# The samples' attention between a state-space stage: where its tiny copies run

## The chip, the cores and the metric

One NeuronCore of one Trainium2 chip runs the kernel. The metric is the device time of one execution in microseconds. The kernel before takes 1613.56 us, the median of three runs (1612.72 to 1615.05).

Engine names as in the profile: PE is the matrix engine (PEld its weight loads), DVE the vector engine, ACT the scalar engine, POOL the general engine (GpSimd), SP the engine that only starts transfers. Each engine runs its own instructions strictly in order; they wait for one another through semaphores.

## The reference

The kernel computes one layer of a decoder trunk for a prompt of 1024 positions and for 8 sample sequences of one new position each. What matters here is the samples' attention over 1024 cached positions (8 pages of 128) and the state-space branch beside it:

```python
z = q @ k.T * HEAD_DIM ** -0.5 + sb_bias         # 16 heads of 64 dims, keys in pages
log_w = log_beta + reverse_cumsum(log_keep) - log_keep   # stick-breaking, no softmax
o_att = exp(log_w) @ v

bu = einsum("gpc,bsgc->bsgp", bb, u)             # 64 groups, complex state of 64
x  = associative_scan(affine, (abar, bu))        # along the 1024 positions
y  = einsum("gcp,bsgp->bsgc", c, x) + d_skip * u
g  = gelu(y)
y_ssm = (g * sigmoid(g @ w_glu + b_glu) * silu(gate)) @ w_ssm_out

merged = sigmoid(m_att) * y_att + sigmoid(m_ssm) * y_ssm
x <- LayerNorm(alpha * x + gate(c) * (merged @ w_out))
```

Everything is float32; a product of matrices is made of three passes with split operands (ahi by whi, alo by whi, ahi by wlo).

## The kernel before

The program is in stages. First come the modulation, the projections and the prompt's attention (to some 715 us). Then the **state-space stage** (to about 1130 us): PE goes through the remaining column blocks of the input projection (`pj`, L141), and between them works on the eight feature blocks of the state-space branch. For each feature block, `take` (L970) has ACT evacuate the SSM input u out of PSUM in three chunks; two `inputs` matmuls (`sps`) are evacuated by ACT into the state tiles sr and si (L999, L1000); `recur` has DVE rotate them and run eight scans in place (L1028), and form xs (L1037); PE multiplies xs (`yp`, L1048); and `gelu` (L1080 to L1085) goes back and forth: ACT makes gh, gq and the polynomial's factor (L1080 to L1082), DVE the product gq·gh (L1083), ACT the tanh (L1084), DVE the result yy (L1085). There are two gelus to a feature block. Gate chunks (L1520) are evacuated by ACT too. After it come the merge, the gated linear unit and the projection `ssm_out` (to about 1340 us), the attention's output projection, and the finish.

The **samples' attention** is spread through the state-space stage. `SampleAttention.todo` is a list of small steps, and `tick` takes a few off it at each step of PE's work. K comes in 16 tiles of eight dims by four pages, V in eight tiles; a tile is `s_t`, of which there are two buffers. A "load" step is a pacing copy of one column into the tile (L805) and then four indirect transfers that POOL starts (L807). A K step handles two dims: two tiny copies make the factor tile s_q (L818, L819), and two operations (L828) add page times factor into the scores s_sc. A V step copies the pacing column into the accumulator (L815) and does two weighted sums (L823).

**Pacing.** `k.last` is a column of whatever the stage wrote last: u, sr, gin or the gelu's gh in the state-space stage. A copy from it makes the step depend on that work, so that a scheduler, which orders the instructions of each engine except PE by a simulated timeline, cannot put the step before it. PE's order is written out by hand. SP starts most weight loads; POOL starts the page loads, and makes the low parts of weights (wlo, L109).

The **late values** (`LateValues`, from some 1184 to 1337 us) are the part of the samples' V pages that are left for later: 32 tiles l_t, four buffers, loaded two steps ahead. `load` is a pacing copy from the column l_p (L865) and an indirect transfer by POOL (L866); each step then multiplies the tile (L884) and reduces it (L885) on DVE. At the end DVE adds the pages' sums (L888) and ACT's queue stores the result as d_o, which is read back as `orow` (L1283) and transposed by PE (L1285).

Of the kernel before, what the change touches and what calls it, by code (L numbers as in the profile page):

```python
# [9 lines left out]
F32 = mybir.dt.float32  # L10
# [136 lines left out]
class Stream:  # L147
# [33 lines left out]
    def one(self):  # L181

        if self.cur is None and self.begun:
            self.cur, self.n = self.begun.popleft()
        if self.cur is None:
            if not self.jobs:
                return False
            self.cur, self.n = gemm(self.k, *self.jobs.popleft()), 0
        next(self.cur)
        self.n += 1  # L190
        self.left -= MM
        self.clock += MM
        last = self.n == KT * 9
        if last:
            self.cur = None
            self.k.w.ensure()
        self.due()
        return None if last else True
# [41 lines left out]
def modulate(k, sp, ps, io, tabs):  # L240
# [28 lines left out]
    def turn(g):  # L269
# [7 lines left out]
        for i in range(2):  # L277
# [4 lines left out]
            k.act_h.append(split_act(k, k.hp, x))  # L282

    load(0)
    bc = sp.tile([128, 16], F32, name="bc", bufs=1)
    SP.dma_start(bc, io["bc"])
# [6 lines left out]
    k.w.stage.append(k.w2)  # L293
    k.w.ensure()
    load(1)
    next(tabs)
    load(2)
    SP.dma_start(k.ident, io["ident"])
    SP.dma_start(k.hb, io["sb_bias"].broadcast_to((128, H)))
# [447 lines left out]
class SampleAttention:  # L747
# [50 lines left out]
    def one(self, what, hf=0, c=0, d0=0):  # L798
        k, nc, pool = self.k, self.k.nc, self.pool
        DVE = nc.vector  # L800
        if what == "load":
            what, hf, c = hf, c, d0
            self.tiles.append(pool.tile([128, 4, 8, 128], F32, tag="s_t", bufs=2, name="s_t"))
            tile = self.tiles[-1]
            DVE.tensor_copy(tile[:, 0, 0, 0:1], k.last)  # L805
            for j in range(4 if what == "k" else VP):
                nc.gpsimd.indirect_dma_start(  # L807
                    out=tile[:, j].rearrange("p d s -> p (d s)"), out_offset=None, in_=self.io["cache_" + what],
                    in_offset=bass.IndirectOffsetOnAxis(ap=self.idx[:, 4 * hf + j, c:c + 1], axis=0))
        elif what in "kv":  # L810
            pages = 4 if what == "k" else VP
            sc = self.sc[:, 4 * hf:4 * hf + pages]
            dd = 8 * c + d0
            if what == "v":
                DVE.tensor_copy(self.acc[:, hf, dd:dd + 1], k.last)  # L815
            else:
                q = pool.tile([128, 2], F32, tag="s_q2", bufs=2, name="s_q2")
                DVE.tensor_copy(q[:, 0:1], k.last)  # L818
                DVE.tensor_copy(q, self.q[:, dd:dd + 2])  # L819
            for d in range(d0, d0 + 2):  # L820
                t, dd = self.tiles[0][:, 0:pages, d], 8 * c + d
                if what == "v":
                    DVE.scalar_tensor_tensor(t, t, 1.0, sc, op0=ALU.mult, op1=ALU.mult,  # L823
                                             accum_out=self.acc[:, hf, dd:dd + 1])
                elif dd == 0:
                    DVE.tensor_scalar(sc, t, q[:, 0:1], None, op0=ALU.mult)
                else:
                    DVE.scalar_tensor_tensor(sc, t, q[:, d - d0:d - d0 + 1], sc, op0=ALU.mult, op1=ALU.add)  # L828
            if d0 == 6:
                self.tiles.popleft()  # L830
        elif what == "w":
            n = PPS * 128
            ke = pool.tile([128, n], F32, tag="s_t", bufs=2, name="s_ke")
            sc = self.sc.rearrange("p j s -> p (j s)")
            nc.scalar.activation(ke, sc, AF.Sigmoid, bias=self.bias[:, 1:2], scale=-0.125)
            nc.scalar.activation(sc, sc, AF.Sigmoid, bias=self.bias[:, 0:1], scale=0.125)
            rev = ke[:, ::-1]
            DVE.tensor_tensor_scan(rev, rev, k.zcol.broadcast_to((128, n)), 1.0, ALU.mult, ALU.add)
            DVE.tensor_tensor(sc[:, 0:n - 1], sc[:, 0:n - 1], ke[:, 1:n], ALU.mult)
            nc.sync.dma_start(k.d_sc, sc[:, 128 * VP:])  # L840
        else:
            nc.sync.dma_start(k.d_acc, self.acc[:, 0])


class LateValues:
# [16 lines left out]
    def load(self, j, c):  # L862
        k, nc = self.k, self.k.nc
        t = self.ld.tile([128, 8, 128], F32, tag="wc", bufs=4, name="l_t")
        nc.vector.tensor_copy(t[:, 0, 0:1], k.last)  # L865
        nc.gpsimd.indirect_dma_start(  # L866
            out=t.rearrange("p d s -> p (d s)"), out_offset=None, in_=self.io["cache_v"],
            in_offset=bass.IndirectOffsetOnAxis(ap=self.idx[:, VP + j, c:c + 1], axis=0))
        self.tiles.append(t)
# [320 lines left out]
class Merge:  # L1190
# [77 lines left out]
    def open_a(self):  # L1268

        k, nc = self.k, self.k.nc  # L1270
        self.a_guard = self.pool("seta", "right")
        pa = self.a_guard.__enter__()
        self.act_a = []

        def one(f):
            t = self.load(k.d_a[f, 0], "x", NP)
            o, s = (self.ld.tile([128, NP], F32, tag="wc", bufs=4, name=n) for n in ("olo", "sga"))
            nc.sync.dma_start(o, k.d_a[f, 1])
            nc.sync.dma_start(s, k.d_sa[f])
            nc.vector.tensor_tensor(t[:, 0:NP], t[:, 0:NP], o, ALU.add)  # L1280
            nc.vector.tensor_tensor(t[:, 0:NP], t[:, 0:NP], s, ALU.mult)
            ob = self.ld.tile([NS, 128], F32, tag="orow", bufs=2, name="orow")
            nc.sync.dma_start(ob, k.d_o[:, blk(f)])  # L1283
            tp = k.psg.tile([128, 512], F32, tag="g", name="otp")
            nc.tensor.transpose(tp[:, 0:NS], ob, k.ident[0:NS, 0:NS])  # L1285
            nc.vector.tensor_tensor(t[:, NP:NT], tp[:, 0:NS], k.sgs[:, f], ALU.mult)
            self.act_a.append(split_act(k, pa, t))

        return [(110, None, lambda f=f: one(f)) for f in range(KT)]
# [429 lines left out]
```

## Time and profile before

| | |
|---|---|
| median of three runs | 1613.56 us (1612.72 to 1615.05) |
| the profiled execution | 1617.42 us, its span 1615.7 us |
| mean granted clock of PE | 0.969 |
| busy: PE, DVE, POOL, ACT | 1489.5, 1218.9, 911.0, 736.5 us |
| pacing and factor copies of the samples' attention on DVE | L805 24, L818 64, L819 64 |
| pacing copies of the late values on DVE | L865 32 |
| score operations L828 | 126 in 114.0 us, mean 905 ns |

In the profile's rows "out<-in" are tile names, and a bracket gives the idle time of the engine just before the row and what ended it: "[8.72 <-ACT u L970]" says that the engine stood for 8.72 us until ACT's instruction of line 970 on tile u was done. A row of the waits gives their total in us, their number and the longest. A row of a group of one form gives the duration's minimum, median and maximum in ns, then the first and last start.

### The profile page before, as it was taken

The numbers are of one execution on the slowest core, as the hardware profiler recorded it, in microseconds if no ns is written. First come the engines' busy times: TensorE is split into PE (matmuls) and PEld (weight loads), VectorE is DVE, ScalarE is ACT, GpSimd is POOL, SyncE is SP. The second block draws the span as 40 slices with busy tenths as digits, with TensorE's granted clock in tenths as the row PEclk, the third lists the DMA queues.
The fourth block names the chain that finished last, engine by engine and source line by source line (L and its number), as shares of the span: only waits on it lengthen the run. The fifth ranks groups of instructions, "written<-read, shape, count | busy, mean of one in ns | idle before, by whom it ended". The sixth has DMA issues, their size and how long they took to land.

```text
span 1615.7 us, 25524 instructions
## 1 busy us (share of the span) xinstructions
PE 1489.5 (92%) x9321; PEld 1410.2 (87%) x9321; DVE 1218.9 (75%) x1717; ACT 736.5 (46%) x1360; POOL 911.0 (56%) x744
## 2 busy tenths in 40 slices
PE   8899999999999999999989978889979786999997
PEld 4789999999999998999888978889779685899885
DVE  5558888888888888743899978787489975744566
ACT  3557777777776776643433333333432212311200
POOL 1738787878777877766566555552176541132164
PEclk9899999999999999999999989999989997999999
DMA  9323433334343434348789887875546677954322
GB/s 356 111 82 89 104 100 97 99 97 113 87 113 93 115 88 111 101 123 288 246 266 287 265 265 249 285 235 132 164 158 222 213 249 261 348 180 140 118 79 91
DMA packets 176731, 275.47 MB, mean 170 GB/s; under 512 B 46395, under 2 KB 119867, under 8 KB 176477
## 3 DMA queue, kind: packets, MB, share of 16 engines
q1 hardware_dynamic: 150555, 180.40, 36.6%
q0 software_dynamic: 23456, 84.95, 16.4%
q10 hardware_dynamic: 2594, 8.49, 2.0%
q8 instruction: 73, 1.20, 0.3%
q14 instruction: 53, 0.43, 0.1%
HBM read 196.77 MB, written 66.24 MB: 163 GB/s over the span
## 4 chain that ended last, share of the span: by engine, by line
PE 49%; DVE 26%; DMA 9%; issue 5%; ACT 3%; POOL 2%; SPq 1%; DVEq 0%; ACTq 0%; POOLq 0%
PE pj L141 32%; PE f L1397 6%; DVE s_sc L828 4%; PE o L700 3%; PE z L654 3%; PE tp L683 3%; DVE ke L665 3%; DVE l_t L884 2%; DMA s_t<-in_cache_k,s_idx 2%; DVE be L666 2%; DVE vs L636 2%; DMA l_t<-in_cache_v,l_idx 2%; DVE l_acc L885 2%; DVE wlo L109 1%; DVE xs L1037 1%
## 5 line engine op out<-in xcount | busy, mean ns | idle before, releaser
L141 PE MATMUL pj<-ahi,whi 128*128 128x344 f32 x2112 | 695.4, 331 | 36.8 <-ACT u L970 17.5
L141 PE MATMUL pj<-alo,whi 128*128 128x344 f32 x2112 | 686.1, 326 | 7.9 <-DVE alo L1220 4.1
L141 PE MATMUL pj<-ahi,wlo 128*128 128x344 f32 x2112 | 581.6, 328 | 6.0 <-POOL wlo L109 6.0
L141 PEld LDWEIGHTS pj<-ahi,whi 128*128 128x128 f32 x2112 | 405.6, 192 | 45.9 <-ACT u L970 18.3
L141 PEld LDWEIGHTS pj<-alo,whi 128*128 128x128 f32 x2112 | 405.6, 192 | 11.9 <-DVE alo L235 4.9
L141 PEld LDWEIGHTS pj<-ahi,wlo 128*128 128x128 f32 x2112 | 382.6, 192 | 8.0 <-POOL wlo L109 6.5
L665 DVE TENSOR_TENSOR_SCAN ke<-ke,eye 128x896 f32<-128x896 f32 (+7 forms) x128 | 217.7, 1701 | 92.4 <-ACT ke L655 92.2
L109 POOL TENSOR_TENSOR wlo<-w,whi 128x1024 fp32r<-128x1024 f32 x53 | 141.6, 2672 | 207.7 <-ACT whi L108 178.8
L108 ACT CAST whi<-w 128x1024 fp32r<-128x1024 f32 x90 | 94.9, 1055 | 137.3 <-PE pj L141 100.1
L655 ACT ACTIVATE ke<-z,nhb 128x448 f32<-128x448 f32 (+2 forms) x192 | 111.8, 582 | 81.1 <-PE z L654 79.2
L666 DVE TENSOR_TENSOR be<-be,ke 128x896 f32<-128x896 f32 (+7 forms) x128 | 128.0, 1000 | 13.0 <-ACT wthi L686 0.5
L828 DVE SCALAR_TENSOR_TENSOR s_sc<-s_t,s_q,s_sc 128x512 f32<-128x512 f32 x126 | 114.0, 905 | 18.0 <-DMA s_t<-in_cache_k,s_idx 12.0
L656 ACT ACTIVATE be<-z,hb 128x448 f32<-128x448 f32 (+2 forms) x192 | 110.6, 576 | 0.0
L807 POOL DMA_INDIRECT s_t<-in_cache_k,s_idx x64 | 70.6, 1103 | 50.8 <-DVE s_sc L828 15.5
L683 PE MATMUL tp<-ident,be 128*128 128x128 f32 x576 | 88.9, 272 | 0.0
L493 POOL TENSOR_TENSOR pt<-tab 128x256 f32<-128x256 f32 x64 | 79.5, 1241 | 3.1
L492 POOL TENSOR_TENSOR pr<-tab 128x256 f32<-128x256 f32 x32 | 25.9, 811 | 89.4 <-DMA tab<-d_tab 78.7
L1520 ACT ACTIVATE gate<-pj 128x344 f32<-128x344 f32 x72 | 32.7, 458 | 95.4 <-PE pj L141 86.5
L109 DVE TENSOR_TENSOR wlo<-w,whi 128x1024 fp32r<-128x1024 f32 x37 | 62.5, 1689 | 15.4 <-ACT whi L108 15.3
L686 ACT CAST wthi<-tp 128x512 fp32r<-128x512 f32 x96 | 56.7, 590 | 32.3 <-PE tp L683 29.9
L654 PE MATMUL z<-kl,qs 128*128 128x448 f32 (+2 forms) x192 | 66.0, 344 | 4.0 <-DMA kl<-kl 4.0
L687 DVE TENSOR_TENSOR wtlo<-tp,wthi 128x512 fp32r<-128x512 f32 x96 | 65.3, 680 | 5.7 <-ACT wthi L686 5.7
(314 smaller groups left out, 2758.5 us busy)
## 6 DMA issues: line engine op xcount, KB each, us to landing
w<-in_w_in SPq DMA_DIRECT2D x38, 512.0 KB
w<-in_w_in POOLq DMA_DIRECT2D x26, 512.0 KB, 5.6
wc<-in_w_cond SPq DMA_DIRECT2D x24, 512.0 KB
d_a<-ox SPq DMA_DIRECT2D x128, 64.0 KB
gst<-d_gg SPq DMA_DIRECT2D x8, 576.0 KB
x<-in_xr SPq DMA_DIRECT2D x9, 512.0 KB
xt<-in_xt SPq DMA_DIRECT2D x8, 516.0 KB
d_sg<-gate SPq DMA_DIRECT2D x8, 516.0 KB
```

Source lines behind the costliest of these rows:

```text
L108: nc.scalar.copy(whi, w32)
L109: self.eng.tensor_tensor(wlo, w32, whi.bitcast(F32), ALU.subtract)
L141: PE.matmul(ps[c], w[:, blk(t)], x[:, cs(c)], start=(t == 0 and i == 0), stop=(t == KT - 1 and i == 2))
L493: POOL.tensor_tensor(t1, c, d, ALU.mult)
L654: nc.tensor.matmul(z[:, 0:wide], st["q", h][:, blk(i)], x[:, s:s + wide], start=j == 0, stop=j == 1)
L655: nc.scalar.activation(ke[:, s:s + cw], z[:, 0:cw], AF.Sigmoid, bias=k.nhb[:, hd:hd + 1], scale=-0.125)
L656: nc.scalar.activation(be[:, s:s + cw], z[:, 0:cw], AF.Sigmoid, bias=k.hb[:, hd:hd + 1], scale=0.125)
L665: nc.vector.tensor_tensor_scan(rev, rev, self.eye[:, NP - n:][:, ::-1], 0.0, ALU.mult, ALU.add)
L666: nc.vector.tensor_tensor(be, be, ke[:, 1:n + 1], ALU.mult)
L683: PE.transpose(tp[:, 2 * order[a] + e], w[e][:, blk(2 * j + a)], k.ident)
L828: DVE.scalar_tensor_tensor(sc, t, q[:, d - d0:d - d0 + 1], sc, op0=ALU.mult, op1=ALU.add)
L1397: PE.matmul(pp[c], a[:, token(i)], w[:, blk(c, 512)], start=(t == 0 and a is ah and w is wh), stop=(t == KT - 1 and a is al))
```

## The change

Three kinds of tiny copies change engine. The pacing copies at page loads, in `SampleAttention.one` and in `LateValues.load`, are made by POOL, which also starts the transfers behind them. The factor copies are made by ACT, and the factor tile holds eight dims (one tile of K) instead of two, still with two buffers, so that the factors of up to 16 dims can stand ready. Nothing of what is computed changes.

```diff
-            DVE.tensor_copy(tile[:, 0, 0, 0:1], k.last)
+            nc.gpsimd.tensor_copy(tile[:, 0, 0, 0:1], k.last)
             for j in range(4 if what == "k" else VP):
                 nc.gpsimd.indirect_dma_start(
...
             else:
-                q = pool.tile([128, 2], F32, tag="s_q2", bufs=2, name="s_q2")
-                DVE.tensor_copy(q[:, 0:1], k.last)
-                DVE.tensor_copy(q, self.q[:, dd:dd + 2])
+                if d0 == 0:
+                    self.q8 = pool.tile([128, 8], F32, tag="s_q2", bufs=2, name="s_q2")
+                q = self.q8[:, d0:d0 + 2]
+                nc.scalar.copy(q[:, 0:1], k.last)
+                nc.scalar.copy(q, self.q[:, dd:dd + 2])
...
     def load(self, j, c):
         k, nc = self.k, self.k.nc
         t = self.ld.tile([128, 8, 128], F32, tag="wc", bufs=4, name="l_t")
-        nc.vector.tensor_copy(t[:, 0, 0:1], k.last)
+        nc.gpsimd.tensor_copy(t[:, 0, 0:1], k.last)
```

Since the scheduler orders anew, instructions that the diff doesn't name move as well. Lines of the changed kernel from 820 on are those of before plus two. PE's order is the same in both.

**DVE, around the two gelus of the fourth feature block.** s_q_10718 before, and s_q_10682 of the change, are the factors of the same new tile of K. Before:

```order
L1083 TENSOR_TENSOR gq<-gq,gh 128x512
L828 SCALAR_TENSOR_TENSOR s_sc<-s_t,s_q_10625,s_sc 128x512
L828 SCALAR_TENSOR_TENSOR s_sc<-s_t,s_q_10641,s_sc 128x512
L1085 SCALAR_TENSOR_TENSOR yy<-gq,gh 128x512
L828 SCALAR_TENSOR_TENSOR s_sc<-s_t,s_q_10641,s_sc 128x512
L805 COPY s_t<-gh 128x1
L818 COPY s_q_10718<-gh 128x1
L818 COPY s_q_10734<-gh 128x1
L819 COPY s_q_10718<-s_q 128x2
L819 COPY s_q_10734<-s_q 128x2
L828 SCALAR_TENSOR_TENSOR s_sc<-s_t,s_q_10718,s_sc 128x512
L1083 TENSOR_TENSOR gq<-gq,gh 128x512
```

The change, same place:

```order
L1085 TENSOR_TENSOR gq<-gq,gh 128x512
L830 SCALAR_TENSOR_TENSOR s_sc<-s_t,s_q_10510,s_sc 128x512 x2
L1087 SCALAR_TENSOR_TENSOR yy<-gq,gh 128x512
L830 SCALAR_TENSOR_TENSOR s_sc<-s_t,s_q_10510,s_sc 128x512 x2
L1085 TENSOR_TENSOR gq<-gq,gh 128x512
L830 SCALAR_TENSOR_TENSOR s_sc<-s_t,s_q_10682,s_sc 128x512
L1087 SCALAR_TENSOR_TENSOR yy<-gq,gh 128x512
```

The second product (L1083, now L1085) stood behind the first operation on the new tile and now stands ahead of it. In the fifth feature block the order before is the same (L1083 behind the first operation with s_q_11203), and the change there reads:

```order
L1085 TENSOR_TENSOR gq<-gq,gh 128x512
L830 SCALAR_TENSOR_TENSOR s_sc<-s_t,s_q_11004,s_sc 128x512 x2
L1087 SCALAR_TENSOR_TENSOR yy<-gq,gh 128x512
L1085 TENSOR_TENSOR gq<-gq,gh 128x512
L830 SCALAR_TENSOR_TENSOR s_sc<-s_t,s_q_11158,s_sc 128x512
```

There too the second product precedes the first operation on the new tile, whose factors are s_q_11158.

**ACT, the fourth feature block of the change**, from the last evacuations of the state tiles to the first gelu. Before, none of the rows L820 and L821 was there:

```order
L1001 COPY sr<-sps 64x272
L1002 COPY si<-sps 64x272
L1522 ACTIVATE gate<-pj 128x344 x2
L108 CAST whi<-w_10389 128x1024
L1522 ACTIVATE gate<-pj 128x344
L820 COPY s_q_10342<-sr 128x1 x4
L821 COPY s_q_10342<-s_q 128x2 x4
L1522 ACTIVATE gate<-pj 128x344 x2
L108 CAST whi<-w_10545 128x1024
L1522 ACTIVATE gate<-pj 128x344
L939 COPY gin<-tp 128x512
```

Eight copies, four of which read sr, stand between two groups of gate evacuations. sr is also what DVE's scans write.

On POOL a row L805 now stands ahead of the four L807 of each page load, and in the late values a row L867 ahead of each transfer L868, where before the copies stood in DVE's order.

## The prediction

> **What bounds the kernel now.** I read the page first (busy time and chain), then busy time by stage, then the waits of the stage that the change edits, then the timelines around the largest of them.
>
> ```profile
> PE 1489.5 (92%) x9321; PEld 1410.2 (87%) x9321; DVE 1218.9 (75%) x1717; ACT 736.5 (46%) x1360; POOL 911.0 (56%) x744
> PE 49%; DVE 26%; DMA 9%; issue 5%; ACT 3%; POOL 2%; SPq 1%; DVEq 0%; ACTq 0%; POOLq 0%
> ```
>
> TensorE (PE) bounds the whole, and VectorE (DVE) carries a quarter of the chain that ended last. The average hides two different stages. The rows below are 50 us each, busy time of PE, PEld, DVE, ACT and POOL, then the granted clock and the DMA share; the first two lie in the state-space stage with the samples' attention between it, the last two in the stage of the late values.
>
> ```profile
> 900.00:950.00 50.00, 41.28 (x268) 40.15 (x267) 40.15 (x79) 15.83 (x30) 28.73 (x29) 0.90 0.81 262
> 950.00:1000.00 50.00, 45.88 (x300) 44.75 (x299) 43.38 (x79) 20.11 (x37) 23.74 (x24) 0.97 0.77 251
> 1200.00:1250.00 50.00, 49.06 (x302) 48.78 (x303) 49.41 (x53) 12.21 (x17) 32.86 (x19) 0.97 0.60 198
> 1250.00:1300.00 50.00, 36.61 (x207) 35.67 (x206) 47.77 (x58) 12.17 (x17) 24.35 (x15) 0.86 0.66 214
> ```
>
> In the first two PE is busy 41 to 46 of 50 us and DVE 40 to 43, so PE is held up by single waits there, not by a full DVE; ScalarE (ACT) has 30 us free in each. In the late stage DVE is full (49.4, 47.8) and PE is what waits. The waits between 700 and 1100 us, engine, what waited, for whom, total, times, longest:
>
> ```profile
> PE pj L141 <- ACT u L970: 17.5, 4, 8.7
> PE yp L1048 <- DVE xs L1037: 9.9, 4, 3.5
> ACT gq L1084 <- DVE gq L1083: 60.2, 14, 8.7
> ```
>
> PE's largest wait is for ACT's evacuation of the SSM input u (L970), and two of its four times make 12.84 of the 17.5 us. What stands behind them is seen on three engines:
>
> ```profile
> 922.70 1.01 POOL L807 DMA_INDIRECT s_t<-in_cache_k,s_idx  x1 [1.61 <-DVE s_q L819]
> 929.30 0.72 ACT L1082 ACTIVATE gq<-gq,g 128x512 f32<-128x512 f32 x1
> 936.40 0.75 DVE L828 SCALAR_TENSOR_TENSOR s_sc<-s_t,s_q,s_sc 128x512 f32<-128x512 f32 x1 [5.46 <-DMA s_t<-in_cache_k,s_idx]
> 937.07 0.80 DVE L1083 TENSOR_TENSOR gq<-gq,gh 128x512 f32<-128x512 f32 x1
> 937.90 0.63 ACT L1084 ACTIVATE gq<-gq 128x512 f32<-128x512 f32 x1 [7.87 <-DVE gq L1083]
> 940.04 0.66 PE L141 MATMUL pj<-ahi,whi 128*128 128x344 f32 x1 [8.72 <-ACT u L970]
> 944.46 0.32 PE L141 MATMUL pj<-ahi,whi 128*128 128x344 f32 x1
> 944.62 0.32 PE L141 MATMUL pj<-alo,whi 128*128 128x344 f32 x1
> ```
>
> ACT had the factor of the second gelu ready at 930.02. DVE's product for it (L1083) stood behind the first score step of a page that landed at 936.4, since its load could start only at 922.7 when the tile came free. So DVE idled 5.46 us with the product queued, ACT stood 7.87 us with u behind it, and PE idled 8.72 us. After that the matmuls run slow: the 14 from 940.04 to 944.46 take 4.42 us where the pitch of the next two, 0.16 us, would make 2.2, another 2.2 us lost. One cycle later the same happens again:
>
> ```profile
> 980.45 0.72 ACT L1082 ACTIVATE gq<-gq,g 128x512 f32<-128x512 f32 x1
> 985.52 0.75 DVE L828 SCALAR_TENSOR_TENSOR s_sc<-s_t,s_q,s_sc 128x512 f32<-128x512 f32 x1 [4.29 <-issue]
> 986.19 0.68 DVE L1083 TENSOR_TENSOR gq<-gq,gh 128x512 f32<-128x512 f32 x1
> 986.90 0.63 ACT L1084 ACTIVATE gq<-gq 128x512 f32<-128x512 f32 x1 [5.73 <-DVE gq L1083]
> 989.04 0.65 PE L141 MATMUL pj<-ahi,whi 128*128 128x344 f32 x1 [4.12 <-ACT u L970]
> 992.28 0.31 PE L141 MATMUL pj<-ahi,wlo 128*128 128x344 f32 x1
> ```
>
> Here PE loses 4.12 us, and the 11 matmuls up to 992.28 take 3.24 us where 1.76 would do: 1.5 more.
>
> **The change part by part.** It takes 152 tiny copies off DVE in this stage (24 at L805, 64 at L818, 64 at L819) and 32 in the late stage (L865). Minimum, median and maximum in ns:
>
> ```profile
> L818 DVE COPY s_q<-sr x22: 122/142/155, 751.8 to 969.7; 128x1 f32<-128x1 f32 x22
> L819 DVE COPY s_q<-s_q x64: 151/162/2353, 739.7 to 990.6; 128x2 f32<-128x2 f32 x64
> L865 DVE COPY l_t<-l_p x32: 134/142/154, 1184.4 to 1323.5; 128x1 f32<-128x1 f32 x32
> L972 ACT COPY us_s<-pj x8: 213/232/267, 664.6 to 1041.5; 128x8 f32<-128x8 f32 x8
> L1038 POOL COPY xf<-xs x8: 183/192/667, 777.6 to 1116.3; 128x8 f32<-128x8 f32 x8
> 922.46 0.15 DVE L805 COPY s_t<-gin 128x1 f32<-128x1 f32 x1
> 922.53 0.16 DVE L819 COPY s_q<-s_q 128x2 f32<-128x2 f32 x1
> 922.60 0.15 DVE L818 COPY s_q<-gin 128x1 f32<-128x1 f32 x1
> ```
>
> A copy's row says 0.14 to 0.16 us, but in sequence they start 0.07 us apart (922.46, 922.53, 922.60), and up to 0.12 where one waits on the other. So 152 of them are 11 to 18 us of DVE's time, about 15, spread over 350 us that are not full: as plain relief they are worth little. The nearest rows for them elsewhere are 0.232 us on ACT and 0.192 us on POOL, for 8 elements; below lies DVE's 0.07. I take the upper ones: 128 × 0.232 = 29.7 us on ACT, and 56 × 0.192 = 11 us on POOL, both engines with room.
>
> The Trainium skill ("VectorE: DVE Perf Modes", the section on the TRN2 errata) speaks against this trade: it gives a ScalarE operation on SBUF a fixed 224 cycles at 1.2 GHz and a VectorE one 58 at 0.96 GHz, an estimate of 0.19 against 0.06 us, so that ACT pays three times what DVE saves. The rows agree (0.232 against a pitch of 0.07). By it the relief is 9 us rather than 15 and the sum about 1 us worse.
>
> *The two gelu stalls.* What the change does on the path is order (the listings in the section on the change show it). With the copies gone, the second product stands in DVE's new order ahead of the score step that waits for the page, in both cycles. First cycle: DVE is free at about 930.4, so product done 931.1; in the rows above PE starts 2.14 us after ACT takes L1084 (940.04 − 937.90), so PE starts at about 933.2 instead of 940.04: 6.8 us less. The four factor copies that stand on ACT ahead of L1084 fall into the time in which it waits for DVE. Second cycle: L1082 ends at 981.17, product at 981.9, u evacuated by 984.0; PE was ready at 984.92: all 4.12 us go. With the slow matmuls (2.2 + 1.5) that is 6.8 + 4.1 + 3.7 = **−14.6 us**. Bounds: 0 if PE only meets the wait later, −16.5 if all goes. The page still lands at 936.4; what is late next is the score steps themselves, and the next scan queued behind them.
>
> On the slow matmuls the Trainium skill ("TensorE: Matmul & The Clock Gate", the part on the HAM clock gate) says the array falls to half its rate after an idle window of about 3.4 us. The trace agrees: after 8.72 and 4.12 us the pitch was 0.29 us, and it came back within 4.4 and 3.2 us. By that rule a remaining wait of 1.9 us costs only itself, as the sum has it.
>
> *Waits of PE for xs* (9.9 us, 4 times): four to eight copies stood ahead of each xs on DVE, 0.3 to 0.9 us a time: **−2 us** (0 to −5).
>
> *New on ACT.* Copies stand between the chunks of u and, where the pacing value is the state tile sr, ahead of the gate evacuations; such a copy waits until DVE's scan has written sr. The rows are the scans of sr as a group (minimum, median, maximum in ns), then in one cycle the four scans and the gate chunk that will stand behind the copies:
>
> ```profile
> L1028 DVE TENSOR_TENSOR_SCAN sr<-r,sr x32: 390/394/2876, 763.2 to 1107.8; 128x128 f32<-128x128 f32 x32
> 903.44 3.94 DVE L1028 TENSOR_TENSOR_SCAN sr<-r,sr 128x128 f32<-128x128 f32 x4
> 910.45 0.46 ACT L1520 ACTIVATE gate<-pj 128x344 f32<-128x344 f32 x1 [8.17 <-PE pj L141]
> ```
>
> The scan ends at 907.38, eight copies later (1.9 us) it is 909.3, and the gate was due at 910.45: it just fits. Between the chunks of u two to four copies cost 0.3 to 0.9 us a time. Together **+3 us** (1 to 15; the upper end is a rival below).
>
> *What comes back.* In the first cycle of the stage the new order puts two score steps, which wait for a page, ahead of the scan's first products: +1.5 us. And PE arrives some 9 us early at work that the pages pace: their loads move only as far as DVE frees tiles. One page wait of 4.3 to 5.5 us, as in the rows above, comes back nearly whole: +4.5. **+6 us** (0 to 10).
>
> *Late values.* Rows of 1180 to 1340 us, and of the chain's last load:
>
> ```profile
> POOL l_t L866 <- DVE l_t L865: 31.9, 14, 7.0
> DVE l_t L884 <- DMA l_t<-in_cache_v,l_idx: 8.8, 7, 3.4
> 1309.66 0.95 POOL L866 DMA_INDIRECT l_t<-in_cache_v,l_idx  x1 [6.98 <-DVE l_t L865]
> 1309.25 0.20 DVE L865 COPY l_t<-l_p 128x1 f32<-128x1 f32 x2
> 1336.98 0.21 DVE L888 TENSOR_TENSOR l_acc<-l_acc 128x64 f32<-128x64 f32 x1
> PE otp L1285 <- DMA orow<-d_o: 17.2, 1, 17.2
> ```
>
> POOL stood 31.9 us because the pacing copy that lets it load stood in DVE's queue behind other work. Made by POOL itself, the copy goes as soon as the tile is free; of the 6.98 us ahead of the load at 1309.66 I take half, since the tile too has to come free. DVE then gains 32 × 0.07 to 0.1 = 2.2 to 3.2 us of copies and part of its 8.8 us for pages. At the end PE waits 17.2 us for the sum of these values (L888 at 1336.98, stored, loaded as orow), so that gain reaches PE: **−4 us** (0 to −8).
>
> Sum: −14.6 − 2 + 3 + 6 − 4 = −11.6 us. The profiled execution took 1617.42 us, which gives 1605.8; it lies 3.9 us above the median of the runs, 1613.56, and I give the same difference there: **1602 us**.
>
> **The rivals.**
> A. *The stalls move.* The pages set the pace of the score steps; PE, 10 us ahead, waits for the next xs instead. For it: the two stalls end at a page that lands no earlier. Against it: DVE is busy only 40 to 43 of 50 us there, so it can catch up. Only the late values and the faster clock stay: −4 and about a third of the 14.6, with the +3 on ACT: 1613.6 − 6 = 1608 (1603 to 1614).
> B. *Slower: ACT stands on the scan.* From the point where the scan's end plus the copies' 1.9 us passes the gate's due time (the margin above is 1.1 us), the gate chunk is late, its PSUM bank too, and PE waits, past 4 us with 1.5 to 2.2 us of slow matmuls as in the two rows above. There are five such cycles. A scan of sr takes 0.39 to 2.9 us a chunk, and once the gelu stalls are gone PE comes earlier and the margin shrinks. Three cycles at 5 to 6 us are +17, against the −11.6: 1619 (1615 to 1624). Against it: DVE waits for PE's own products before it scans, so the scan moves forward with PE.
> C. *The copies cost more than they free.* ACT's 29.7 us lie in front of evacuations; if a quarter delays PE (7.4 us instead of 3) and DVE's relief brings nothing (2 less): 1608, up to 1615. The skill's section on the errata, above, is the rule behind it.
>
> **How the numbers follow.** Forecast 0.56, its own range 1594 to 1609; A 0.20, B 0.16, C 0.08. This kernel's runs lie within 0.2% of each other, 3.2 us; that is what can be told from no change, so faster means below 1610.3 and slower above 1616.8. Faster: 0.53 + 0.11 + 0.04 = 0.68; same: 0.03 + 0.08 + 0.02 + 0.03 = 0.16; slower: 0.01 from A, 0.14 from B, 0.01 from C = 0.16. The low end has nothing coming back (−6: 1596) and the whole late gain (−4 more): 1592. The high end reaches into the middle of B: 1617.
>
> **What would show it.** Right: PE's wait for u around 930 and 980 us is below 2 us where it was 8.72 and 4.12, with no slow matmuls behind it; DVE's second product there (L1085 in the new numbering) starts within 1 us of the end of its factor on ACT; the wait for orow is below 15 us. Wrong: a new wait of PE for a gate chunk with ACT idle in front of a factor copy (B), a longer wait for xs with DVE idle for a page (A), or u chunks further apart on ACT with DVE no earlier (C).

## The result, and the profile after

The change runs in 1605.12 us (median of four runs, 1604.05 to 1606.17) against 1614.3 us for the kernel before beside it: ratio 0.994, 95% interval 0.9924 to 0.9956, **9.2 us faster**. The forecast was 1602 us with a range of 1592 to 1617, from 1613.56. The sign and nearly the size came out; where the time went did not, as follows.

The profiled execution took 1604.94 us, 12.5 us less than that of before. PE's order is the same in both kernels, so the start of each PE instruction can be set against that of the same instruction before. The differences, in us, at a few places (start before, start after; from the timelines of PE):

| the PE instruction | before | after | difference |
|---|---|---|---|
| near the end of the prompt's attention (o, L700) | 457.46 | 453.35 | −4.1 |
| first yp of the state-space stage | 776.86 | 774.30 | −2.6 |
| the u wait of the third block | 888.14 | 886.89 | −1.3 |
| the first stall of the prediction, one matmul of it | 940.04 | 931.11 | −8.9 |
| the second stall, three matmuls on | 990.07 | 979.71 | −10.4 |
| xs of the sixth block | 1021.26 | 1017.10 | −4.2 |
| last block's yp, end of the stage | 1115.79 | 1113.07 | −2.7 |
| late values, second half | 1247.49 | 1252.49 | +5.0 |
| transposition of orow (otp) | 1347.17 | 1339.51 | −7.7 |
| attention's output projection | 1381.17 | 1368.72 | −12.4 |

The first 4.1 us arise before anything that the change touches (PE, DVE, ACT and POOL have the same instructions in the same order up to there), so they are the chance of these two executions; at 735 us the twelve other changed kernels of this document lie between 4.6 us ahead and 2.8 us behind. From there to the end of the state-space stage the change *loses* 1.4 us; from there to the end it gains 9.8. So in the change the state-space stage gave nothing that can be told from chance, and the late values and what follows them all of it.

The page of after, and PE's waits between 700 and 1145 us:

```profile
PE 1494.4 (93%) x9321; PEld 1413.0 (88%) x9321; DVE 1191.5 (74%) x1533; ACT 748.9 (47%) x1488; POOL 941.4 (59%) x800
```

```profile
PE pj L141 <- ACT u L972: 11.1, 4, 4.1
PE yp L1050 <- DVE xs L1039: 9.6, 4, 3.9
PE pj L141 <- ACT gate L1522: 7.0, 2, 4.6
```

The wait for u fell from 17.5 to 11.1 us only, the wait for xs not at all (9.9 to 9.6), and that for gate chunks rose from 4.2 to 7.0. The timelines show which (PE, in order of time):

```profile
837.41 0.66 PE L141 MATMUL pj<-ahi,whi 128*128 128x344 f32 x1 [3.68 <-ACT u L972]
886.89 0.42 PE L141 MATMUL pj<-ahi,whi 128*128 128x344 f32 x1 [4.08 <-ACT u L972]
933.75 0.42 PE L141 MATMUL pj<-ahi,whi 128*128 128x344 f32 x1 [0.30 <-ACT us_s L974]
979.02 0.43 PE L141 MATMUL pj<-ahi,whi 128*128 128x344 f32 x1 [3.17 <-ACT u L972]
995.44 0.42 PE L141 MATMUL pj<-ahi,whi 128*128 128x344 f32 x1 [2.32 <-ACT gate L1522]
```

Before, the two blocks ahead of the stalls had these waits:

```profile
841.79 0.43 PE L141 MATMUL pj<-ahi,whi 128*128 128x344 f32 x1 [1.50 <-ACT u L970]
888.14 0.43 PE L141 MATMUL pj<-ahi,whi 128*128 128x344 f32 x1 [3.12 <-ACT u L970]
```

The first stall is gone (8.72 us, now 0.30 at its place). The second kept 3.17 of its 4.12 us, the two blocks before grew from 1.50 and 3.12 to 3.68 and 4.08, and the wait for a gate chunk at 995 is new. Its cause, on ACT:

```profile
990.97 1.15 ACT L837 ACTIVATE s_ke<-s_sc,s_bias 128x1024 f32<-128x1024 f32 x1 [8.77 <-DVE s_sc L830]
994.93 0.81 ACT L1522 ACTIVATE gate<-pj 128x344 f32<-128x344 f32 x2
```

The sigmoid over all scores waits for DVE's last score step, and the gate evacuations stand behind it: with PE ten microseconds ahead and the pages not, ACT stood 8.77 us there (3.48 before). The late stage, waits of 1180 to 1340 us of the change, then PE's wait for weight parts before and the last sum of the late values in the change:

```profile
PE pj L141 <- POOL wlo L109: 11.3, 5, 4.7
DVE l_t L886 <- DMA l_t<-in_cache_v,l_idx: 10.9, 6, 2.5
POOL l_t L867 <- DVE l_acc L887: 17.2, 10, 6.2
PE otp L1287 <- DMA orow<-d_o: 4.8, 1, 4.8
```

```profile
PE pj L141 <- POOL wlo L109: 6.0, 2, 3.1
```

```profile
1328.35 0.22 DVE L890 TENSOR_TENSOR l_acc<-l_acc 128x64 f32<-128x64 f32 x1
```

POOL no longer waits for a copy on DVE (31.9 us before) but 17.2 us for the reductions that free a tile; the weight parts that POOL makes in the same queue are later for PE, 11.3 us instead of 6.0. Against that stands the last sum, done at 1328.6 us instead of 1337.2, and with it the wait for orow: 4.8 us instead of 17.2.

### The profile page after: what moved, and what is told of

Same layout as the page of the kernel before. It is cut to its first block, busy times and chain, and to the rows that moved or that the text cites. A ratio compares the mean times of both kernels' runs of the same rounds, so it can differ in the third digit from the quotient of the medians.

```text
span 1603.2 us, 25584 instructions
## 1 busy us (share of the span) xinstructions
PE 1494.4 (93%) x9321; PEld 1413.0 (88%) x9321; DVE 1191.5 (74%) x1533; ACT 748.9 (47%) x1488; POOL 941.4 (59%) x800
## 5 line engine op out<-in xcount | busy, mean ns | idle before, releaser
L141 PE MATMUL pj<-ahi,whi 128*128 128x344 f32 x2112 | 697.2, 331 | 29.3 <-ACT u L972 11.1
L141 PE MATMUL pj<-ahi,wlo 128*128 128x344 f32 x2112 | 583.4, 329 | 11.3 <-POOL wlo L109 11.3
L141 PEld LDWEIGHTS pj<-ahi,whi 128*128 128x128 f32 x2112 | 406.7, 193 | 39.3 <-ACT u L972 12.4
L141 PEld LDWEIGHTS pj<-ahi,wlo 128*128 128x128 f32 x2112 | 383.6, 193 | 14.1 <-POOL wlo L109 12.8
L665 DVE TENSOR_TENSOR_SCAN ke<-ke,eye 128x896 f32<-128x896 f32 (+7 forms) x128 | 225.1, 1758 | 92.9 <-ACT ke L655 92.8
L830 DVE SCALAR_TENSOR_TENSOR s_sc<-s_t,s_q,s_sc 128x512 f32<-128x512 f32 x126 | 117.6, 934 | 27.0 <-DMA s_t<-in_cache_k,s_idx 22.0
L666 DVE TENSOR_TENSOR be<-be,ke 128x896 f32<-128x896 f32 (+7 forms) x128 | 117.1, 915 | 13.0 <-DVE ke L665 0.5
L807 POOL DMA_INDIRECT s_t<-in_cache_k,s_idx x64 | 71.6, 1118 | 29.4 <-issue 14.0
L493 POOL TENSOR_TENSOR pt<-tab 128x256 f32<-128x256 f32 x64 | 76.2, 1190 | 3.1
L654 PE MATMUL z<-kh,qs 128*128 128x448 f32 (+2 forms) x192 | 66.3, 345 | 0.9
```

The lines of the kernel that those rows point to most:

```text
L141: PE.matmul(ps[c], w[:, blk(t)], x[:, cs(c)], start=(t == 0 and i == 0), stop=(t == KT - 1 and i == 2))
L654: nc.tensor.matmul(z[:, 0:wide], st["q", h][:, blk(i)], x[:, s:s + wide], start=j == 0, stop=j == 1)
L665: nc.vector.tensor_tensor_scan(rev, rev, self.eye[:, NP - n:][:, ::-1], 0.0, ALU.mult, ALU.add)
L666: nc.vector.tensor_tensor(be, be, ke[:, 1:n + 1], ALU.mult)
L807: nc.gpsimd.indirect_dma_start(out=tile[:, j].rearrange("p d s -> p (d s)"), out_offset=None, in_=self.io["cache_" + what], in_offset=bass ...
```

## The experiments

Ratios are against the kernel before, run beside each kernel on the same chip, with 95% intervals. Two columns are read from the profiles as in the table above: by how much PE's lead over the kernel before changed between 735 and 1116 us of that kernel's time (the state-space stage), and from 1116 us to the end; negative is a gain. Each of these two columns compares two single executions. The four kernels whose late part is that of before still show −3.0 to +0.3 us in the last column, and the two whose state-space stage is that of before −1.0 and −2.1 in the one ahead of it, so differences of some 3 us there mean nothing.

| kernel | ratio | interval | stage | late and end |
|---|---|---|---|---|
| the change | 0.994 | 0.9924 to 0.9956 | +0.9 | −9.8 |
| late copies only on POOL | 0.9951 | 0.9934 to 0.9967 | −1.0 | −12.8 |
| the change without its late part | 1.0031 | 1.0015 to 1.0047 | +1.7 | −1.4 |
| factor copies only on ACT | 0.9951 | 0.9932 to 0.9970 | −11.2 | −3.0 |
| page-load copies only on POOL | 1.0059 | 1.0038 to 1.0080 | +2.1 | −2.7 |
| the change, page-load copies left on DVE | 0.9895 | 0.9879 to 0.9911 | −8.8 | −11.9 |
| the change, copy before the last transfer | 0.9949 | 0.9933 to 0.9964 | −0.2 | −11.5 |
| factor copies on ACT, DVE's copy holds all four transfers | 0.9952 | 0.9934 to 0.9969 | −11.0 | +0.3 |
| no factor copies, late copies on POOL | 0.9935 | 0.9913 to 0.9957 | −4.8 | −11.9 |
| the 0.9895 kernel, and POOL reads the pacing column | 0.9903 | 0.9878 to 0.9928 | −7.5 | −11.9 |
| the change, POOL copies from a column made by DVE | 0.9899 | 0.9874 to 0.9924 | −7.8 | −11.5 |
| late copies on POOL, and dummies on DVE | 1.000 | 0.9981 to 1.0019 | −2.1 | +0.4 |
| the 0.9895 kernel, AHEAD = 3 (the same program, see below) | 0.9881 | 0.9856 to 0.9906 | −7.8 | −9.7 |

### Which part does what

Four kernels make one part alone, or leave one out. The late part alone:

```diff
 # the kernel before, in LateValues.load
-        nc.vector.tensor_copy(t[:, 0, 0:1], k.last)
+        nc.gpsimd.tensor_copy(t[:, 0, 0:1], k.last)
```

> The kernel before with only the 32 pacing copies of the late values (L865) made by GpSimd; the samples' attention as before. Theory P, the prediction's account (the state-space stage gives most, the late values 4 us): about -4 us (ratio 0.9975). Theory L, read from the traces side by side (instruction by instruction, PE is as far ahead at the end of the state-space stage as at its start, and gains only after it): nearly the whole of the change's 9 us, ratio 0.994 to 0.996, with the wait for orow near 5 us instead of 17 and new waits for the weights' low part near 11 us.

It measured 0.9951, some 8 us: theory L's number, twice the prediction's 4. The change without this part:

```diff
 # the change, in LateValues.load
-        nc.gpsimd.tensor_copy(t[:, 0, 0:1], k.last)
+        nc.vector.tensor_copy(t[:, 0, 0:1], k.last)
```

> The change without its late part: page-load copies on GpSimd, factor copies on ScalarE in tiles of eight, but L865 left on VectorE. Theory P: -7 to -8 us (ratio 0.9955), since both gelu stalls go. Theory L: 0 within 2 us (ratio 0.999 to 1.001): the stall at 940 goes, but waits of 3 to 4 us stand in the cycles before and after it and the scores' end, paced by the pages, holds ScalarE at the sigmoid.

1.0031: the two other parts together make the kernel a little *slower*, against theory P, and outside theory L's 0.999 to 1.001 too. Taken apart they pull in opposite directions. The factor copies alone:

```diff
 # the kernel before, in SampleAttention.one, the K steps
-                q = pool.tile([128, 2], F32, tag="s_q2", bufs=2, name="s_q2")
-                DVE.tensor_copy(q[:, 0:1], k.last)
-                DVE.tensor_copy(q, self.q[:, dd:dd + 2])
+                if d0 == 0:
+                    self.q8 = pool.tile([128, 8], F32, tag="s_q2", bufs=2, name="s_q2")
+                q = self.q8[:, d0:d0 + 2]
+                nc.scalar.copy(q[:, 0:1], k.last)
+                nc.scalar.copy(q, self.q[:, dd:dd + 2])
```

> Only the factor copies are moved to ScalarE in tiles of eight dims; both kinds of pacing copies stay on VectorE. Theory P: the order of VectorE has the second product ahead of the page in the fourth and fifth blocks, as in the change, so -6 to -8 us. Theory L: within 2 us of no change. If ScalarE's copies cost something in front of the evacuations, slower by 2 to 5 us.

0.9951, theory P's size, and the profile shows why: both stalls of the prediction are below 1.4 us. PE's rows of this kernel:

```profile
842.39 0.66 PE L141 MATMUL pj<-ahi,whi 128*128 128x344 f32 x1 [5.37 <-ACT u L972]
931.02 0.42 PE L141 MATMUL pj<-ahi,whi 128*128 128x344 f32 x1 [1.29 <-ACT u L972]
976.16 0.43 PE L141 MATMUL pj<-ahi,whi 128*128 128x344 f32 x1 [1.35 <-ACT u L972]
1014.37 0.80 PE L1050 MATMUL yp<-xs,gst 128*128 128x128 f32 x2 [7.13 <-DVE xs L1039]
```

The wait of 3.12 us in the third block is gone too; in turn 5.37 us stand in the second, and xs of the sixth block is 7.13 us late. That is the part that comes back. The page-load copies alone:

```diff
 # the kernel before, in SampleAttention.one, a load
-            DVE.tensor_copy(tile[:, 0, 0, 0:1], k.last)
+            nc.gpsimd.tensor_copy(tile[:, 0, 0, 0:1], k.last)
```

> Only the 24 pacing copies at page loads (L805) are made by GpSimd; factor and late copies stay on VectorE. VectorE's order here has the second product ahead of the page in the fourth and fifth blocks too. Theory P: -5 to -8 us, with no load on ScalarE. Theory L: within 2 us of no change, with other waits in place of the two stalls.

1.0059, **slower**, which neither theory had. 24 copies of one column cost 0.6% (9.5 us by the ratio, 6.1 by the medians). In its profile the u waits of the second and third blocks are 5.29 and 4.74 us:

```profile
842.65 0.66 PE L141 MATMUL pj<-ahi,whi 128*128 128x344 f32 x1 [5.29 <-ACT u L970]
891.67 0.65 PE L141 MATMUL pj<-ahi,whi 128*128 128x344 f32 x1 [4.74 <-ACT u L970]
986.00 0.65 PE L141 MATMUL pj<-ahi,whi 128*128 128x344 f32 x1 [2.67 <-ACT u L970]
1002.59 0.55 PE L141 MATMUL pj<-ahi,whi 128*128 128x344 f32 x1 [2.65 <-ACT gate L1520]
```

In DVE's order of this kernel, too, the second product of the fourth and fifth blocks stands ahead of the page. So the order of these two instructions is not enough.

### Without the page-load copies on POOL

```diff
 # the change, in SampleAttention.one, a load
-            nc.gpsimd.tensor_copy(tile[:, 0, 0, 0:1], k.last)
+            DVE.tensor_copy(tile[:, 0, 0, 0:1], k.last)
```

> The change with the page-load pacing copies (L805) left on VectorE: factor copies on ScalarE, late copies on GpSimd. If the two gains measured apart (each ratio 0.995) add up: about 1597 us, ratio 0.990. If the late stage only takes up what the earlier one leaves: 1603, ratio 0.995.

0.9895, 1595.83 us: the two gains add up, and it beats the kernel before by 16 us and the change by some 7. The change is thus two gains of 8 us and one loss of about 7. The rest asks where that loss comes from.

**Is it that POOL's copy stands in front of all four transfers?** On DVE the copy holds back only the transfer into whose place it writes; the other three can go first on POOL. Two kernels, one that lets them go first, and one that makes all four wait for a copy on DVE:

```diff
 # the change, in SampleAttention.one, a load
-            nc.gpsimd.tensor_copy(tile[:, 0, 0, 0:1], k.last)
-            for j in range(4 if what == "k" else VP):
+            for j in [*range(1, 4 if what == "k" else VP), 0]:
+                if j == 0:
+                    nc.gpsimd.tensor_copy(tile[:, 0, 0, 0:1], k.last)
                 nc.gpsimd.indirect_dma_start(
```

> The whole change, but GpSimd starts the three page transfers that the pacing copy doesn't touch first, then makes the copy, then starts the fourth. Theory G (the copy on GpSimd stands in front of all four transfers of a page, where on VectorE it held back only the one into whose place it writes, so pages come later): about as the change with L805 left on VectorE, ratio 0.990 to 0.992. Rival S (the copies on GpSimd themselves cost: 0.2 to 0.7 us each on a busy engine, and VectorE waiting to overwrite sr until GpSimd has read it): as the change, ratio 0.994.

```diff
 # factor copies on ScalarE only; in SampleAttention.one, a load (VP is 4)
-            DVE.tensor_copy(tile[:, 0, 0, 0:1], k.last)
+            DVE.tensor_copy(tile[:, 0:(4 if what == "k" else VP), 0, 0:1], k.last.unsqueeze(1).broadcast_to([128, 4 if what == "k" else VP, 1]))
```

> Factor copies on ScalarE as in the change, pacing copies on VectorE, but each page-load copy writes one column in the place of all four transfers, so that all four wait for it; no copy on GpSimd. Theory G: the gain of the factor copies is lost, ratio 0.999 to 1.004, with VectorE waiting longer for pages. Rival S: no loss, ratio 0.995 as with the factor copies alone.

0.9949 and 0.9952: no gain where three transfers go first, no loss where all four are held. Theory G falls by both. (The listing of the change has the copy ahead of its four transfers at each load. In the trace that is so at 18 of the 24 loads; at the other six the scheduler had put three transfers in front.)

**Is it that POOL reads the pacing column late?** In the change's profile one wait of DVE has POOL's copy as its cause. Rows of POOL and DVE around it:

```profile
943.47 1.21 POOL L807 DMA_INDIRECT s_t<-in_cache_k,s_idx  x1 [6.03 <-DVE s_sc L830]
944.99 0.94 POOL L807 DMA_INDIRECT s_t<-in_cache_k,s_idx  x1 [0.30 <-issue]
946.23 0.94 POOL L807 DMA_INDIRECT s_t<-in_cache_k,s_idx  x1 [0.30 <-issue]
947.18 0.20 POOL L805 COPY s_t<-sr 128x1 f32<-128x1 f32 x1
947.41 0.69 DVE L1023 TENSOR_TENSOR sr<-sr,ec 128x512 f32<-128x512 f32 x1 [3.01 <-POOL s_t L805]
```

The copy reads sr, and DVE rotates sr in place. The copy stands behind three transfers that can start only when DVE has freed the tile (943.47), at 1.2 to 1.5 us each, so DVE idles 3.01 us until POOL has read one column. With the copy on DVE there can be no such wait: DVE is past the copy when it comes to the rotation. Two kernels test it: one adds a late read by POOL where there was none, the other takes it away and keeps POOL's copies.

```diff
 # the 0.9895 kernel, behind the transfers of a load (s_bias has six spare columns)
+            self.turn += 1
+            col = self.bias[:, 2 + self.turn % 6:3 + self.turn % 6]
+            nc.gpsimd.tensor_copy(col, k.last)
```

> The best kernel so far (factor copies on ScalarE, late copies on GpSimd, page-load copies L805 on VectorE; ratio 0.9895) with one more copy on GpSimd at each page load, which reads the pacing column into a spare place; nothing waits for what it writes, and VectorE's order is the same. Theory W (what costs in the change is that GpSimd reads sr late, standing behind the transfers it starts, and VectorE may not overwrite sr until then; traces: VectorE idle 3.0 us once before it overwrites sr, and pages later from there): much of the 8 us between the two is lost again, ratio 0.993 to 0.995. Rival O (the change's loss there comes from the order in which the scheduler puts VectorE's score steps): stays near 0.990. Rival Q (24 more copies in GpSimd's queue, 0.2 to 0.7 us each, delay transfers): also 0.993 to 0.995, but with no wait of VectorE for GpSimd.

```diff
 # the change, in SampleAttention.one, a load
-            nc.gpsimd.tensor_copy(tile[:, 0, 0, 0:1], k.last)
+            self.turn += 1
+            col = self.bias[:, 2 + self.turn % 6:3 + self.turn % 6]
+            DVE.tensor_copy(col, k.last)
+            nc.gpsimd.tensor_copy(tile[:, 0, 0, 0:1], col)
```

> The whole change, but VectorE first copies the pacing column into a spare column, in its own order, and GpSimd's pacing copy reads that one, so that sr is free as soon as VectorE has passed. Theory W: about 0.990. Rival Q (the copies in GpSimd's queue): 0.994, as the change. Rival O: between, by its order.

0.9903 and 0.9899. The second is theory W's number: with POOL's copies in place but sr free early, the whole gain is back. 24 copies in POOL's queue by themselves cost nothing that shows in either (Q falls). The first is not W's number, though it is the cleaner test, since DVE and POOL have the same instructions in the same order as in the 0.9895 kernel, but for the added copies. The wait is there, in the profile of that kernel,

```profile
949.17 0.69 DVE L1027 TENSOR_TENSOR sr<-sr,ec 128x512 f32<-128x512 f32 x1 [3.00 <-POOL s_bias L813]
```

and PE's lead grows less around it (from 900 to 1000 us by 8.2 us, against 12.7 in the 0.9895 kernel), but at the stage's end it is −7.5 against −8.8, and no loss of time can be told within 0.0025. Over the same 100 us the four other kernels in which POOL reads sr gained 8.0 to 10.6 us, and the five with the factor copies on ACT in which it doesn't 10.6 to 12.9. So the wait shows where it stands, in one block, by some 3 us, and theory W, by which it makes the 7 us, fails. The four kernels in which POOL's copy of the stage's own tile paces the pages also lose 2.6 to 7.1 us between 735 and 900 us, where no wait of DVE for such a copy above 0.4 us was seen; the kernel with only the added read loses nothing there.

DVE's waits for K pages do not explain it either: in the stage they are 22.0 us in the change and 11.8 in the 0.9895 kernel, but 24.4 us in the kernel with the column that DVE puts aside, which has the whole gain. And that kernel is not the change with one read less, since the scheduler ordered it anew: DVE's 8.0 us of waiting for POOL's dd early in the stage of the change (7.9 before) is not there, and DVE waits 10.9 us for its first page instead. What is shown is that the loss is gone when the copy stays on DVE, and when POOL's copy reads a column that DVE has put aside. Why the pacing copy on POOL costs 7 us when it reads the stage's own tile, and the same read as an added copy nothing that shows, stays open; rival O, the order that the scheduler makes of it, is neither shown nor ruled out.

### Smaller questions

**No factor copies at all.** The score steps can read s_q itself:

```diff
 # the 0.9895 kernel, the K steps
-                if d0 == 0:
-                    self.q8 = pool.tile([128, 8], F32, tag="s_q2", bufs=2, name="s_q2")
-                q = self.q8[:, d0:d0 + 2]
-                nc.scalar.copy(q[:, 0:1], k.last)
-                nc.scalar.copy(q, self.q[:, dd:dd + 2])
+                q = self.q[:, dd:dd + 2]
```

> As the first of these, but with no factor copies at all: the score steps read s_q itself, and only the page loads pace them. If ScalarE's copies in front of the evacuations of u cost what its waits show (2 to 4 us over the stage): ratio 0.988 to 0.989. If they are hidden: as the first, 0.990. If the looser pacing lets the scheduler put steps in front of the scans: slower than it.

0.9935, slower than 0.9895 with 128 instructions fewer: the third of the outcomes written down. Its reason fits, though nothing else tests it: in DVE's order 13 score steps now stand in a row ahead of the rotation of one block, where the 0.9895 kernel has at most 9.

**What the late gain is.** The same copies again, on DVE, into a column that nobody reads:

```diff
 # late copies only on GpSimd; in LateValues.load
         nc.gpsimd.tensor_copy(t[:, 0, 0:1], k.last)
+        x = self.pool.tile([128, 1], F32, tag="l_x", bufs=4, name="l_x")
+        nc.vector.tensor_copy(x, k.last)
```

> The kernel before with the late pacing copies on GpSimd (ratio 0.995) and in addition the same 32 copies on VectorE into a spare column that nobody reads. If the late gain is that the loads are issued earlier: 0.995 to 0.996. If it is VectorE's relief of 32 copies in a full stage: 0.998 to 1.000.

1.000: 32 idle copies on DVE take the whole gain back, although POOL still paces its own loads. Waits of 1180 to 1360 us, first with the late copies on POOL only, then with the dummies:

```profile
POOL l_t L865 <- DVE l_acc L885: 17.3, 10, 6.3
DVE l_t L884 <- DMA l_t<-in_cache_v,l_idx: 12.8, 7, 2.5
POOL l_t L865 <- DVE l_p L860: 2.4, 1, 2.4
PE otp L1285 <- DMA orow<-d_o: 3.9, 1, 3.9
```

```profile
DVE l_t L886 <- DMA l_t<-in_cache_v,l_idx: 17.3, 10, 3.3
POOL l_t L865 <- DVE l_p L860: 13.6, 5, 5.2
PE otp L1287 <- DMA orow<-d_o: 11.2, 1, 11.2
POOL l_t L865 <- DVE l_acc L887: 11.1, 8, 6.2
```

With the dummies POOL waits 13.6 us for the pacing column l_p (L860), which comes later in DVE's queue, the pages come later (17.3 us instead of 12.8) and with them orow (11.2 instead of 3.9). 32 copies at the pitch of 0.07 to 0.1 us are only 2 to 3 us of DVE; the rest is put down here to what their places in its order do to the column and the loads, which no run separates from the copies' time.

**Loading further ahead.**

```diff
 # the 0.9895 kernel
-AHEAD = 2
+AHEAD = 3
```

> The best kernel so far with the late values loaded three steps ahead instead of two (same four buffers). Where VectorE still waits for pages in the late stage: 1 to 4 us faster than 0.9895, 0.987 to 0.989. If the four buffers or GpSimd's weight work hold the loads: no change, or slower where GpSimd stands on a load in front of the weights' low parts.

0.9881, 1596.5 us, with an interval that holds 0.9895: no difference that can be told. But this edit tested nothing. In the two traces every engine has the same instructions on the same tiles in the same order, so the scheduler, with the same four buffers, made the same program of both. What it gives is a second measurement of one program on another chip: the ratios differ by 0.0014, the two columns of the table by 1.0 and 2.2 us. Whether earlier loads would help stays open.

## Why the prediction was right, and where it was not

**The sum held by luck, through errors that cancel.** −11.6 was forecast and −9.2 measured, but by terms of −7.6 for the state-space stage and −4 for the late values, where the profile has about +1 and −10. The measured 1605 us also lies in the range of rival A (1603 to 1614), so the time alone does not choose between the forecast and A.

- *The two gelu stalls, −14.6.* The mechanism and the size are right for the factor copies: alone, they bring the stalls to 1.29 and 1.35 us, and PE is 12 us further ahead in that kernel from 930 to 1000 us. In the change only the first went; of the second 3.17 us stayed, with matmuls at a pitch of 0.29 us up to 982.6 behind it, against the first sign of being right. (From 940.04 to 944.46 there are 15 slow matmuls, not 14, which makes 2.0 us lost instead of 2.2.)
- *The page-load copies.* This is the step that failed. They were priced at 0.192 us each on an engine "with room" and have no term in the sum. On POOL they took up to 0.70 us each, cost 0.6% by themselves, and about 7 us in the change. The working asked what stands behind the moved copy on its new engine, but not who has to wait until it has *read*: here DVE, which overwrites sr, for 3.01 us in one block. That wait is not the whole of the 7 us, by the kernel with only the added read; the rest of the cause stays open.
- *Waits for xs, −2.* 9.9 to 9.6 us: nothing.
- *New on ACT, +3.* The feared wait came, but off PE's path: ACT stood 22.0 us, five times, in front of a factor copy for DVE's scan of sr, and no gate chunk was late for it: the two that were late had the sigmoid ahead of them (995 us) or were late before (4.22 us at 1087, 4.65 now at 1083). The rows, a group of ACT in the change and what it waited for:

```profile
L820 ACT COPY s_q<-sr x22: 186/188/192, 748.6 to 953.6; 128x1 f32<-128x1 f32 x22
  DVE sr L1030: 22.0, 5
```

- *What comes back, +6.* Right in kind: xs of the sixth block is late by 7.13 us with the factor copies alone, and the sigmoid over the scores holds ACT. Of the lead of 13.5 us at 1000 us in that kernel 1.4 are lost again by 1116 us; in the change 7.2 of 9.9.
- *Late values, −4.* Right in its end and half the size: 8 us alone. That the wait for orow would be below 15 us held (4.8). The way there was another: DVE's wait for these pages did not shrink from 8.8 us but grew, to 10.9 in the change and 12.8 with the late copies alone, and PE first fell back, from 2.7 us ahead to 5.0 behind, before the earlier sum brought it forward. A cost was missed: PE's wait for weight parts from POOL, 11.3 us instead of 6.0.
- *The rivals.* Rival A describes the stage as it came out ("the stalls move"), with another cause: not the pages' pace as such, since with the copies on DVE the same pages let 9 to 11 us through. B did not happen. C is the reverse of what the runs show for the factor copies.

## What to carry to other kernels

When an instruction moves to another engine, ask for each tile that it reads who overwrites it next: that engine can now wait for the mover's place in its new queue, however short the instruction is: 3.0 us here for a copy of 0.2 us. Whether such a wait reaches the end is another question, and here put alone into the 0.9895 kernel it did not show. Move one part at a time: here two parts were worth 0.5% each and the third cost about what one of them brought, and only runs of the single parts told them apart. Before a run is read as a test, see whether the scheduler turned the edit into another order at all. Where two programs keep the order of the bounding engine, set its instructions against each other one by one; a total that agrees with a forecast says little about its terms.

## What the runs showed of the hardware

- **A tiny copy costs its pitch, not its duration, on ACT too.** The factor copies take 0.188 us each, but three in a row take 0.37 us, so they start 0.09 us apart:

```profile
975.17 0.37 ACT L820 COPY s_q<-gh 128x1 f32<-128x1 f32 x3
```

The 29.7 us that the prediction put on ACT would be about 12 if all 128 stood in a row at this pitch, an estimate. The prediction set ACT's duration, 0.232 us, against DVE's pitch, 0.07; pitch against pitch it is 0.09 against 0.07. The Trainium skill ("VectorE: DVE Perf Modes", on the TRN2 errata) gives a fixed 224 cycles at 1.2 GHz for a ScalarE operation on SBUF, an estimate of 0.19 us; that is the duration measured here, and not what one more copy in a row adds.

- **PE's clock can halve after a wait of 2.32 us, and not at once.** The Trainium skill ("TensorE: Matmul & The Clock Gate", the HAM clock gate) names an idle window of about 3.4 us for it. After the wait of 2.32 us at 995.44 the pitch stayed 0.16 us for six matmuls and was then 0.29 us until 999.6; the granted clock was 1.00 from 995.5 to 996.5 and 0.50 from 996.5 to 999.9. Rows of the change:

```profile
996.34 0.32 PE L141 MATMUL pj<-ahi,wlo 128*128 128x344 f32 x1
996.49 0.45 PE L141 MATMUL pj<-ahi,whi 128*128 128x344 f32 x1
996.74 0.49 PE L141 MATMUL pj<-alo,whi 128*128 128x344 f32 x1
997.02 0.49 PE L141 MATMUL pj<-ahi,wlo 128*128 128x344 f32 x1
999.89 0.34 PE L141 MATMUL pj<-ahi,whi 128*128 128x344 f32 x1
```

From 996.49 to 999.89 that is 12 matmuls in 3.40 us where 1.9 would do: this wait of 2.32 us cost 3.8. The prediction had taken such a wait to cost only itself. The wait's length alone does not decide: behind the 3.12 us at 888.14 in the kernel before, the pitch stayed 0.16 us and the granted clock 1.00.

- **A copy of one column on POOL took 0.18 to 0.70 us in the change**, against 0.12 to 0.155 on DVE and 0.184 to 0.204 on ACT. The group of those that read sr, nine of the 24:

```profile
L805 POOL COPY s_t<-sr x9: 188/586/700, 823.0 to 1061.0; 128x1 f32<-128x1 f32 x9
```
